# Cross-covariance attention on one core: one late store in column parts, three others head by head

## The chip, the core and the metric

The kernel runs on one core of a Trainium2 chip. The metric is device time in microseconds of one execution; the number given is the median of three runs. A run that is profiled besides leaves a trace: instructions of all engines, and the packets and landings of the transfers.

## The reference

For 8 batches of 12 heads, with 512 tokens and 64 features in float32, each head's features are normalised over the tokens, correlated with each other, passed through a softmax, and applied to V:

```
Q_norm = Q / (norm(Q, axis=-2) + 1e-10)          # over the 512 tokens
K_norm = K / (norm(K, axis=-2) + 1e-10)
attn = einsum('bhnd,bhne->bhde', Q_norm, K_norm) # 64 x 64 a head
attn = softmax(attn, axis=-1)
out  = einsum('bhnd,bhde->bhne', V, attn)
```

Q, K and V are 12.6 MB each, the output as much: 37.75 MB are read and 12.58 MB written.

## The kernel before

The 96 heads are worked in 12 steps (s = 0 to 11) of 8 heads, two steps to a pair w. A tile has 128 partitions: four heads with 32 partitions each, and a partition holds 16 tokens of each of two such groups of heads; the index r (0 or 1) tells the groups apart, and the kernel's text calls them heads. For each step the kernel loads 1 MB of Q and of K (`load_qk`, lines 219 and 221) and 1 MB of V (`load_v`, line 225), casts them to bf16, squares and sums for the norms, forms the Gram matrices on TensorE, scales them, takes the softmax, transposes V, multiplies, and copies the product from PSUM to an output tile `so[s]` (`ocopy`, line 205 on ScalarE). `so[s]` has the shape 128 x 2 x 16 x 64 (partition, r, token j, feature) in float32: 1 MB. In DRAM the 16 tokens of one partition and one r are 4096 bytes in a row, so a whole store is 256 rows of 4 KB.

The order of all pieces of work is planned ahead by the class `Order`, which lists them by costs, due times and ranks and emits them one by one; each engine then runs its own list in that order. All stores and nearly all loads are issued by SP (SyncE), one after the other. A transfer takes one of eight semaphores in turn, and its issue waits until the transfer that had this semaphore eight places before has landed. There are six output tiles, so that `so[s]` is used again by step s+6.

`store(s, i)` issues the store of step s, in one of three ways. For s = S - SPLIT = 9 it is split: PAR["CUTS"] has for each r the ranges of partitions that leave as transfers of their own, which are 0 to 68 and 68 to 128 for r=0, and all 128 for r=1 (line 232). All other steps leave as one transfer of 128 x 2 x 1024 (line 234), since the planner gives i = None for them. A store waits for the four copies into the part of `so[s]` that it reads. The last four stores, s = 8 to 11, are issued at 106.22, 109.13 (three parts), 111.42 and 114.83 us of the span, and their data wait in the queues of the 16 DMA engines behind what was issued earlier.

Of the kernel before, what the change touches and what calls it, by code (L numbers as in the profile page):

```python
# [13 lines left out]
PAR = {'NB': {'qk': 7, 'v': 3, 'vb': 2, 'qm': 2, 'sq': 2, 'vt': 2, 'so': 6, 'sm': 2, 'ab': 4},  # L14
 'TAIL': 3,
 'FINE': (0,),
 'ACTQ': True,
 'X': 1.27,
 'R': {'ck': 14.3601,
       'q': -46.9145,  # L20
       'sq': -4.5261,
       'sk': 21.309,
# [34 lines left out]
 'V_PACE': 0.7666,  # L57
 'ST_LAG': 6.0835,
 'SPLIT': 3,
 'CUTS': (((0, 68), (68, 128)), ((0, 128),))}  # L60

D = 64
T = 32
# [86 lines left out]
def kernel(  # L150
# [7 lines left out]
    nc = tc.nc  # L158
# [10 lines left out]
    Of = out.rearrange("b h (p j) d -> (b h p) (j d)", j=TT).rearrange("(w r e p) x -> w e p r x", r=2, e=2, p=128)  # L169
# [28 lines left out]
    qk32, qkb, sq, v32, vb, gram, st, s2, nn, r12, kqs, lg, ls, ex, ab, vps, vt, po, so = ({} for _ in range(19))  # L198
# [27 lines left out]

    def store(s, i):
        if s == S - PAR["SPLIT"]:
            for r in range(2):
                o, y = Of[s // 2, s % 2, :, r], so[s][:, r].rearrange("p j d -> p (j d)")  # L230
                for a, b in PAR["CUTS"][r]:
                    nc.sync.dma_start(out=o[a:b], in_=y[a:b])
        elif i is None:
            nc.sync.dma_start(out=Of[s // 2, s % 2], in_=so[s].rearrange("p r j d -> p r (j d)"))
        else:
            nc.sync.dma_start(out=Of[s // 2, s % 2, :, i], in_=so[s][:, i].rearrange("p j d -> p (j d)"))
# [232 lines left out]
    for s in range(S):  # L469
        for x in range(4):  # L470
            n = 4 * s + x - 2
            wait = [("oc", n // 4, n % 4)] if n >= 0 else []
            order = [("ou", s, x - 1) if x else back("ou", s, 1, 3)]
            piece(("ou", s, x), {"PE": 0.56}, [("vc", s // 2, *t) for t in turns(s // 2) if t[0] == x] + [("nm", s)] + wait, order, R["ou"] + 0.01 * s, outs, s, x)
            free = ([("st", s - NB["so"], i) for i in halves(s - NB["so"])] if x == 0 and s >= NB["so"] else [])
            order = [("oc", s, x - 1) if x else back("oc", s, 1, 3)]
            piece(("oc", s, x), {"ACT": 0.6, "DVE": 0.69}, [("ou", s, x)] + free, order, R["oc"] + 0.01 * s, ocopy, s, x)
        last = None
        for i in halves(s):
            order = [("st", s, 0) if i else ("st", s - 1, halves(s - 1)[-1]) if s else None]  # L480
            piece(("st", s, i), {"DMA": 2 * X if i is None else X}, [("oc", s, x) for x in range(4)], order, v_at(0.5 * s) + PAR["ST_LAG"], store, s, i)
# [35 lines left out]
```

## Time and profile before

| | |
|---|---|
| median of three runs | 128.31 us (128.14 to 128.37) |
| the profiled execution | 128.12 us |
| its span, first to last instruction | 126.0 us |
| busy: PE, DVE, ACT, POOL | 65%, 63%, 67%, 37% of the span |
| moved by DMA | 50.59 MB, mean 402 GB/s |
| transfers of SP and ACT (q1 and q10) | 95.3% and 2.0% of 16 engines' span |
| issued stores | 11 of 1024 KB, one of 512, 272 and 240 KB |
| time to landing of a 1024 KB store | 17.4 us median |

The span is the time from the first to the last instruction of the profiled execution; its own time has a start and an end around that. Shares of DMA are shares of 16 DMA engines; a fully loaded window reads slightly above 1, since the records of consecutive packets overlap a little. Engine names are PE (TensorE), DVE (VectorE), ACT (ScalarE), POOL (GpSimd) and SP (SyncE), with a q behind the name for an engine's queue of instructions. L232 is line 232 of the kernel. A landing is the time at which a transfer's semaphore was raised; it is raised once by each DMA engine that took part.

### The profile page before, as it was taken

The page shows a single profiled execution, that of the slowest core. Times are in us where ns is not written, and L with a number is a line of the kernel's source. Part 1 is how long each engine was busy: PE and PEld are TensorE (multiplying, and loading weights), DVE is VectorE, ACT ScalarE, POOL GpSimd, SP SyncE. Part 2 cuts the span into 40 slices and gives each one's busy share as a digit, 9 for nine tenths or more (in the row PEclk, how much of TensorE's full clock was granted, in tenths as well). Part 3 has the DMA queues.
Part 4 walks back from the last instruction along what each step waited for, and adds up shares of the span by engine and source line. Part 5 has one row for each costly group of instructions (what it writes and reads, how often), then busy time and mean ns, then how long its engine had stood idle before and what let it go on. Part 6 is the DMA issues. An engine that isn't in the chain of part 4 may idle for free.

```text
span 126.0 us, 4061 instructions
## 1 busy us (share of the span) xinstructions
PE 81.7 (65%) x1800; PEld 54.2 (43%) x1800; DVE 79.4 (63%) x140; ACT 85.0 (67%) x116; POOL 46.5 (37%) x40
## 2 busy tenths in 40 slices
PE   0009459894598787869578898864799878951000
PEld 0006145571474465557335556451387446630000
DVE  2223343899853989988987599993789998700000
ACT  4086668595697854998799987929839885864000
POOL 3250665470637098062707916144324700000000
PEclk9999999999657999995959999998559999996555
DMA  3999999999999999999999999999999999999982
GB/s 107 416 420 428 432 411 423 421 419 414 430 415 428 416 427 412 419 414 427 414 436 415 416 419 412 442 399 421 433 416 416 411 420 411 419 412 423 406 359 85
DMA packets 11588, 50.59 MB, mean 402 GB/s; under 512 B 819, under 2 KB 819, under 8 KB 10035
## 3 DMA queue, kind: packets, MB, share of 16 engines
q1 hardware_dynamic: 11283, 49.29, 95.3%
q10 hardware_dynamic: 288, 1.05, 2.0%
q8 instruction: 14, 0.23, 0.6%
q14 instruction: 3, 0.02, 0.0%
HBM read 37.75 MB, written 12.58 MB: 399 GB/s over the span
## 4 chain that ended last, share of the span: by engine, by line
DMA 54%; PE 15%; DVE 11%; ACT 6%; SPq 3%; issue 2%; ACTq 0%
DMA qk<-in_Q_dram 31%; DMA v<-in_V_dram 17%; DMA qk<-in_K_dram 6%; PE po L338 4%; ACT so L205 3%; PE l L266 3%; PE gram L260 3%; SPq L225 3%; DVE ab L310 2%; PE vps L323 2%; PE gram L289 2%; DVE s L271 1%; ACT sq L251 1%; DVE vt L207 1%; ACT vb L205 1%
## 5 line engine op out<-in xcount | busy, mean ns | idle before, releaser
L209 POOL TENSOR_SCALAR kb<-qk 128x2048 bf16<-128x2048 f32 (+1 forms) x13 | 23.4, 1802 | 38.1 <-DMA qk<-in_K_dram 35.0
L205 ACT COPY so<-po 128x512 f32<-128x512 f32 x47 | 25.6, 583 | 4.0 <-PE po L338 2.9
L251 ACT ACTIVATE sq<-qb 128x2048 bf16<-128x2048 bf16 (+1 forms) x13 | 23.1, 1778 | 7.7 <-DVE qb L207 7.6
L209 POOL TENSOR_SCALAR vb<-v 128x1024 bf16<-128x1024 f32 x15 | 20.1, 1355 | 13.7 <-DMA v<-in_V_dram 13.7
L338 PE MATMUL po<-ab,vt 128*32 128x128 bf16 x768 | 21.0, 237 | 6.0 <-ACT ex L299 1.6
L260 PE MATMUL gram<-qb,kb 32*128 32x128 bf16 x768 | 15.6, 240 | 12.2 <-POOL kb L209 9.6
L266 PE MATMUL l<-sq,hm 128*32 128x512 bf16 x96 | 19.5, 470 | 1.7 <-ACT sq L251 1.1
L323 PE MATMUL vps<-ident,vb 128*128 128x128 f32 x96 | 17.2, 305 | 4.4 <-POOL vb L209 2.3
L207 DVE CAST qb<-qk 128x2048 bf16<-128x2048 f32 (+1 forms) x12 | 13.6, 1135 | 10.0 <-DMA qk<-in_Q_dram 9.9
L260 PEld LDWEIGHTS <-kb 32*128 32x128 bf16 x768 | 13.4, 106 | 14.3 <-POOL kb L209 10.9
L338 PEld LDWEIGHTS <-vt 128*32 128x32 bf16 x768 | 14.3, 103 | 12.0 <-issue 7.7
L207 DVE COPY vt<-vps 128x1024 bf16<-128x1024 bf16 (+1 forms) x25 | 16.5, 664 | 3.0 <-PE vps L323 2.8
L251 ACT ACTIVATE sq<-kb 128x2048 bf16<-128x2048 bf16 (+1 forms) x10 | 17.3, 1734 | 0.7 <-POOL kb L209 0.7
L205 ACT CAST vb<-v 128x1024 bf16<-128x1024 f32 x9 | 12.1, 1344 | 6.8 <-DMA v<-in_V_dram 6.6
L323 PEld LDWEIGHTS vps<-ident,vb 128*128 128x128 f32 x96 | 11.3, 152 | 8.2 <-POOL vb L209 3.1
L271 DVE TENSOR_REDUCE s<-l 64x128 f32<-64x512 f32 x12 | 8.1, 678 | 8.5 <-PE l L266 8.5
L289 PE MATMUL gram<-ident,kqs 128*128 128x128 f32 x48 | 9.7, 336 | 3.5 <-DVE kqs L285 3.1
L295 DVE TENSOR_TENSOR ls<-gram,r 64x256 f32<-64x256 f32 x24 | 10.1, 420 | 2.7 <-PE gram L289 2.5
L285 DVE TENSOR_TENSOR kqs<-gram,r 128x512 f32<-128x512 f32 x12 | 8.2, 687 | 3.2 <-ACT r L281 2.6
L266 PEld LDWEIGHTS <-hm 128*32 128x32 bf16 x96 | 5.7, 108 | 9.7 <-issue 7.8
L310 DVE TENSOR_TENSOR ab<-ex,rb 128x512 bf16<-128x512 f32 x12 | 9.4, 781 | 0.4
L289 PEld LDWEIGHTS gram<-ident,kqs 128*128 128x128 f32 x48 | 6.2, 166 | 7.5 <-DVE kqs L285 6.6
(25 smaller groups left out, 41.3 us busy)
## 6 DMA issues: line engine op xcount, KB each, us to landing
v<-in_V_dram SPq DMA_DIRECT2D x12, 1024.0 KB, 19.5
qk<-in_Q_dram SPq DMA_DIRECT2D x11, 1024.0 KB, 19.6
qk<-in_K_dram SPq DMA_DIRECT2D x11, 1024.0 KB, 19.7
out_dram<-so SPq DMA_DIRECT2D x11, 1024.0 KB, 17.4
qk<-in_K_dram ACTq DMA_DIRECT2D x2, 512.0 KB, 6.0
qk<-in_Q_dram SPq DMA_DIRECT2D x2, 512.0 KB, 5.7
out_dram<-so SPq DMA_DIRECT2D x1, 512.0 KB, 10.0
out_dram<-so SPq DMA_DIRECT2D x1, 272.0 KB
```

The lines of the kernel that those rows point to most:

```text
L205: nc.scalar.copy(o, i)
L207: nc.vector.tensor_copy(o, i)
L209: nc.gpsimd.tensor_scalar(out=o, in0=i, scalar1=1.0, scalar2=0.0, op0=ALU.mult, op1=ALU.add)
L251: nc.scalar.activation(o, i, AF.Square)
L260: nc.tensor.matmul(gram[s][:, h, 0], k, q, start=(t == 0), stop=(t == TT - 1))
L266: nc.tensor.matmul(st[s][32 * x:32 * (x + 1)].rearrange("p t d -> p (t d)"), hm, sq[s][:, x, t:t + 4].rearrange("p t r d -> p (t r d)"), s ...
L271: nc.vector.tensor_reduce(out=s2[s], in_=st[s].rearrange("p t d -> p d t"), axis=mybir.AxisListType.X, op=ALU.add)
L289: nc.tensor.transpose(gram[s][:, h, 1], kqs[s][:, h], ident)
L295: nc.vector.tensor_tensor(out=ls[s][half], in0=gram[s][half, :, 1, half], in1=r12[s][half, :HU, None].to_broadcast([D, HU, D]), op=ALU.mult)
L310: nc.vector.tensor_tensor(out=ab[s], in0=ex[s][:, :, None, :].to_broadcast([128, HU, 2, D]), in1=rb[:, :, :, None].to_broadcast([128, HU, ...
L323: nc.tensor.transpose(ps[:, n], vb[w][:, j].rearrange("p r d c -> p (r d c)").bitcast(F32), ident)
L338: nc.tensor.matmul(po[s, x][32 * h:32 * (h + 1), j].rearrange("p r d -> p (r d)"), v, ab[s][:, h].rearrange("p r d -> p (r d)"), start=Tru ...
```

## The change

The split store of s=9 is cut anew, by tokens as well as partitions. A cut is now (r, first token, end token, first partition, end partition): tokens 0 to 6 of r=0 leave for the partitions 0 to 124 and 124 to 128 apart, then tokens 6 to 16 of r=0 for all 128 partitions, and then r=1 whole. The stores of the steps 8, 10 and 11 leave in two transfers each, first r=0 and then r=1. The planner doesn't know of this, and its order is unchanged. SP issues four transfers more; the lists of the other engines stay as they are.

```diff
  'SPLIT': 3,
- 'CUTS': (((0, 68), (68, 128)), ((0, 128),))}
+ 'HALF': (8, 10, 11),
+ 'CUTS': ((0, 0, 6, 0, 124), (0, 0, 6, 124, 128), (0, 6, 16, 0, 128), (1, 0, 16, 0, 128))}
...
     def store(s, i):
         if s == S - PAR["SPLIT"]:
+            for r, j0, j1, a, b in PAR["CUTS"]:
+                nc.sync.dma_start(out=Of[s // 2, s % 2, a:b, r, j0 * D:j1 * D], in_=so[s][a:b, r, j0:j1].rearrange("p j d -> p (j d)"))
+        elif s in PAR["HALF"]:
             for r in range(2):
-                o, y = Of[s // 2, s % 2, :, r], so[s][:, r].rearrange("p j d -> p (j d)")
-                for a, b in PAR["CUTS"][r]:
-                    nc.sync.dma_start(out=o[a:b], in_=y[a:b])
+                nc.sync.dma_start(out=Of[s // 2, s % 2, :, r], in_=so[s][:, r].rearrange("p j d -> p (j d)"))
         elif i is None:
             nc.sync.dma_start(out=Of[s // 2, s % 2], in_=so[s].rearrange("p r j d -> p r (j d)"))
```

The new rows of s=9 are 1536 bytes long for the tokens 0 to 6, and 2560 bytes for the tokens 6 to 16; together they are the 4096 bytes of before.

## The prediction

> **What bounds the kernel now.** I read the page first (engines, slices), then the chain of waits, then the waits of SP's queue, then single transfers and narrow time windows at the end. No engine is busy for more than 67% of the span, while the DMA line stands at 9 from the second slice on:
>
> ```profile
> PE 81.7 (65%) x1800; PEld 54.2 (43%) x1800; DVE 79.4 (63%) x140; ACT 85.0 (67%) x116; POOL 46.5 (37%) x40
> ...
> DMA  3999999999999999999999999999999999999982
> ```
>
> The chain's last piece of computing is the copy of the last output tile, and what SP waits for after that is only the landing of stores:
>
> ```profile
> 114.22 0.58 ACT so L205
> ```
>
> ```profile
> SPq L512 <- DMA out_dram<-so: 9.7, 1, 9.7
> ```
>
> So computing ends at 114.80 us and the last 11 us are the DMA engines emptying what is queued. The span ends 1.1 us after the last landing (below). What can shorten this kernel here is only how evenly the last megabytes lie over the 16 DMA engines. Time windows of that stretch (columns: window, its length, busy PE, PEld, DVE, ACT, POOL, granted clock, share of the 16 DMA engines, GB/s):
>
> ```profile
> 119.00:120.00 1.00, 0.00 (x0) 0.00 (x0) 0.00 (x0) 0.00 (x0) 0.00 (x0) 0.50 1.02 418
> ...
> 121.00:121.50 0.50, 0.00 (x0) 0.00 (x0) 0.00 (x0) 0.00 (x0) 0.00 (x0) 0.50 0.86 352
> ...
> 122.50:123.00 0.50, 0.00 (x0) 0.00 (x0) 0.00 (x0) 0.00 (x0) 0.00 (x0) 0.50 0.72 295
> ...
> 123.50:124.00 0.50, 0.00 (x0) 0.00 (x0) 0.00 (x0) 0.00 (x0) 0.00 (x0) 0.50 0.29 115
> 124.00:124.50 0.50, 0.00 (x0) 0.00 (x0) 0.00 (x0) 0.00 (x0) 0.00 (x0) 0.50 0.08 33
> ```
>
> A full load reads 1.02. So three engines run dry before 121 us, two more before 122.5, most of the rest between 123.5 and 124, and one or two are left in the last half microsecond. The trace's landing records, one time for each DMA engine of a transfer, say it exactly. The last store (s=11) lands on three engines at 121.04 to 121.19, on two at 122.71 and 122.80, on nine at 123.90 to 124.25, and on two alone at 124.64 and 124.89. The two late ones are what the change can reach.
>
> **Whose engines they are.** Store s=9, the one that is cut, was issued in three parts; SP's timeline gives their start, the DMA issues their size and time to landing:
>
> ```profile
> 109.13 1.18 SPq L232 DMA_DIRECT2D out_dram<-so  x3
> 111.42 3.79 SPq L234 DMA_DIRECT2D out_dram<-so  x2
> ```
>
> ```profile
> out_dram<-so SPq DMA_DIRECT2D x1, 512.0 KB, 10.0
> out_dram<-so SPq DMA_DIRECT2D x1, 272.0 KB
> out_dram<-so SPq DMA_DIRECT2D x1, 240.0 KB, 9.1
> ```
>
> In the landing records the 68-row part has 4 engines' landings (117.08, 117.21, 117.73, 117.80; the other 12 counts come with the issue at 109.58, hence no time in the list), the 60-row part 15, a 128-row part 16. That is the greatest divisor of the rows that is not above 16. So in s=9 four engines ("the four") carry 17+4+8 = 29 rows of 4 KB, eleven carry 4+8 = 12, and one carries 8. Store s=8 before it had landed on seven engines at 114.32 to 115.14, three at 115.84 to 115.94 and six at 117.06 to 117.45. The four start from the early seven (117.08 less 17 rows is 114.4, 117.80 less 17 rows is 115.2), and followed through 60-row part, second head, s=10 and s=11, two of them are the stragglers: 117.80, 118.66, 119.92, 122.40, 124.89, and 117.73, 118.41, 119.66, 122.16, 124.64. The six late engines of s=8 are in the nine and end at up to 124.25. Today the four have been given about half a microsecond too much.
>
> **Price of a row.** The packet records give 159 ns for 4096 bytes, 309 ns for 8192 and 9 ns for a completion: 9 ns a packet and 150 ns per 4 KB. Consecutive packets overlap a little: 16 rows with their completion take 2.49 us (118.92 to 121.41 to 123.90), 155.4 ns a row. So I take 5.4 + 150 x bytes/4096 ns: 61.7 ns for 1536 bytes, 99.2 for 2560, 155.4 for 4096. No row of 1536 or 2560 bytes is in this trace. The lower bound is bytes alone (58.3 and 97.1), the upper within this line the whole packet time (65.3 and 102.8); a rival below goes beyond it.
>
> **The change, part by part.**
>
> *Cut of s=9.* 124 and 4 rows go to 4 engines each by the same count: 31+1 rows of 1536 bytes, then 8 rows of 2560 and 8 of 4096 on all 16. The four: 32 x 61.7 + 8 x 99.2 + 8 x 155.4 = 1.97 + 0.79 + 1.24 = 4.01 us, against 29 x 155.4 = 4.51: 0.50 less (bounds 0.43 to 0.62). The eleven: 0.79 + 1.24 = 2.04 against 12 x 155.4 = 1.86: 0.17 more (0.16 to 0.19). The one: 2.04 against 1.24, 0.79 more, hidden: it belongs to the three that end at 121.
>
> The Trainium skill, "DMA: Bandwidth & Descriptors", section "Why a DMA increments its semaphore by 16 and not by 1", has the same count of engines for 68, 60 and 128 rows as the landing records, and adds what no record here names, that SP's transfers take the lowest-numbered engines, so that both pieces would fall on the four that the 68-row part used; by that the sum stays at 127.87.
>
> *Stores 8, 10 and 11 by heads, and one part more in s=9.* The bytes per engine are the same, and rows stay 4 KB. Added are three completions on most engines, four on the four, 9 ns each: 0.03 and 0.04 us. A gap between two transfers is not seen: 8 rows of the second head of s=9 took 1.24 us from landing to landing, half of the 2.49 of a whole store. SP issues four more transfers (0.33 to 0.40 us each), while it would wait anyway. The semaphore of each transfer is reused eight transfers later, so now the last ones wait for nearer landings: s=10's heads for s=6 and s=7 (112.40 and 114.91, where s=10 left at 111.42), s=11's heads for the two heads of s=8 (about 116.2 and 117.45, where s=11 left at 114.83). Nothing stands behind them on SP but the end. What hides this is the queue: from the first issue to its first packet it takes 1.0 us (0.74 to 1.75), so the last head is ready by about 118.9 with its issue, and the emptiest engine needs it at 114.32 + 2.04 + 2.49 + 1.24 = 120.1, the late ones at 123.2. If that cover were gone, each microsecond of late issue past it would count in full. Cost taken: nothing. The instructions of PE, DVE, ACT and POOL are the same in the same order; the output tiles of these stores are not reused.
>
> *Sum.* Stragglers: 124.89 - 0.50 + 0.04 = 124.43. The late engines: 124.25 + 0.17 + 0.03 = 124.45, now the last. The end moves from 124.89 to 124.45: 0.44 us (0.39 to 0.49 by the bounds; what a cheaper row would give beyond this, the late engines keep). The profiled execution took 128.12 us (126.0 span, 2.1 around it), so 127.68; the median of the runs lies 0.19 above that execution: **127.87**.
>
> The Trainium skill speaks against the change, in "DMA: Bandwidth & Descriptors", section "Rules for kernel authors": small transfers should be joined, and below 64 KB one pays mostly overhead; the first head's 4-row piece is 6 KB. The 60-row part of 240 KB shows none of it here (landings 0.62 us after s=8's on the late engines, four rows' time), but no run here shows a 6 KB one.
>
> **The rivals.**
>
> *Late engines alone set the end.* One straggler lost 0.25 us at 115.76, where a foreign packet of 8 KB (314 ns, the instruction queue q14) fell on it. If that falls elsewhere in ordinary runs, before ends at 124.64 there, after still at 124.45: a gain of 0.2, 128.1. For it: the runs spread by 0.23 us. Against: the profiled execution has the packet and is no slower than they are.
>
> *Short rows cost more than their bytes (slower).* Place: the 32 rows of 1536 bytes on the four. From 76 ns a row on the stragglers end after 124.89. At 100 ns they take 3.20 instead of 1.97 us: 129.1; if every packet cost as much as one of 4 KB, 48 x 155.4 = 7.46 against 4.51: 131.3. For it: no such row is measured. Against: the 4096, 8192 and 4-byte packets lie on one line.
>
> *The pieces land on other engines (slower).* If they fell on four of the late ones, those would carry 4.05 instead of 1.86 us and end at 126.4: 129.9. Nothing in the trace hints at a rotation, but it has one such transfer only.
>
> *The added transfers leave gaps (slower).* Where a transfer began only as after an idle queue, 1.0 us each, three more on the late engines would give 131.3; from 0.15 us each on it is slower. Against: a share of 1.02 across all the boundaries from 114 to 120 us. This is what the rule on small transfers of the Trainium skill ("DMA: Bandwidth & Descriptors", "Rules for kernel authors") would amount to.
>
> *The 124 rows are spread over 16 engines after all,* so the change does not shift load as said: the late ones get 8 x 61.7 ns more and end near 124.95: 128.4, no change.
>
> **How the numbers follow.** Less than 0.2% (0.26 us) can't be told from no change. Forecast 0.64; late engines alone 0.14; short rows 0.08; other engines 0.05; gaps 0.05; spread 0.04. Faster: the forecast and a part of the second, 0.67; same: 0.14; slower: 0.19. The range: the forecast's own is 127.7 to 128.0 with the runs' spread; up to 128.5 it takes in the second and the last rival and mildly dear rows, down to 127.6 a foreign packet that falls well.
>
> **What would show it.** Right: the last landing at about 124.45, all four parts of s=9 with landings on 4, 4, 16 and 16 engines, packets of 1536 bytes at about 65 ns, eleven or more engines ending within half a microsecond, and a steeper fall of the DMA share after 123.5. Wrong: packets of 1536 bytes above 85 ns; a share below 1 between 114 and 120 us; stragglers among the engines that were late in s=8 by more than 0.2 us; s=11's second head issued later than 119.

## The result, and the profile after

The changed kernel takes 127.55 us (median of six runs, 127.52 to 127.77), the kernel before 128.16 us beside it (six runs, 128.02 to 128.37): the ratio is 0.9953, with a 95% interval from 0.9940 to 0.9966. That is faster by 0.61 us, where 0.44 was forecast, and 0.05 us below the lower end of the range. The profiled execution took 127.52 us with a span of 125.4, against 128.12 and 126.0. Ratios and their intervals, here and below, are worked out from the single runs and not from the two medians, so they can differ from the quotient of the medians. Two slow runs, one of e1_cut_only (130.20 us) and one of the kernel before (130.32 us, beside e5 to e7), are left out of them.

The page after shows the same picture: no engine busy for more than 68%, and the DMA line full but for its ends.

```profile
PE 77.8 (62%) x1800; PEld 52.3 (42%) x1800; DVE 81.1 (65%) x140; ACT 84.8 (68%) x116; POOL 47.0 (37%) x40
...
DMA  2999999999999999999999999999999999999993
```

The chain of waits ends with the same copy, at 114.82 us (114.80 before), so nothing was gained ahead of the last stores:

```profile
114.23 0.59 ACT so L206
```

The time windows of the end (window, length, busy engines, granted clock, share of 16 DMA engines, GB/s):

```profile
119.00:120.00 1.00, 0.00 (x0) 0.00 (x0) 0.00 (x0) 0.00 (x0) 0.00 (x0) 0.50 1.03 422
...
121.00:121.50 0.50, 0.00 (x0) 0.00 (x0) 0.00 (x0) 0.00 (x0) 0.00 (x0) 0.50 0.94 385
...
122.50:123.00 0.50, 0.00 (x0) 0.00 (x0) 0.00 (x0) 0.00 (x0) 0.00 (x0) 0.50 0.71 287
...
123.50:124.00 0.50, 0.00 (x0) 0.00 (x0) 0.00 (x0) 0.00 (x0) 0.00 (x0) 0.50 0.50 205
124.00:124.50 0.50, 0.00 (x0) 0.00 (x0) 0.00 (x0) 0.00 (x0) 0.00 (x0) 0.50 0.03 8
```

Before, the share was 0.29 from 123.5 to 124 and 0.08 after that: by the landing records, two engines were left over. Now it is 0.50 and then 0.03: more engines work to the end, and they stop nearly together. By the landing records the last head of s=11 lands on three engines at 121.56 to 121.99, two at 122.96 and 123.11, the four at 123.55, 123.61, 124.13 and 124.35, and seven at 124.40 to 124.55. The last landing came 0.34 us earlier (124.89 to 124.55).

The span, however, became 0.60 us shorter, so another 0.26 us lies behind the last landing. SP's own waits show where (waiting line, releaser, us in total, times, longest):

```profile
SPq L514 <- DMA out_dram<-so: 6.5, 5, 1.8
```

Before it was one wait of 9.7 us. At its end SP checks the eight transfer semaphores with five waiting instructions, always in the same order. Before, the last store's semaphore was in the first of them: SP waited there until 124.91, and then the other four, all long satisfied, ran at 124.98, 125.05, 125.11 and 125.17. The four transfers that were added move the last store on to the semaphore in the fifth: the first four waits are done at 119.66, 120.88, 122.09 and 123.32, while the queue is still emptying, and only one is left at 124.56. The span ends 0.84 us behind the last landing instead of 1.10.

SP's timeline of the end and its DMA issues, to be held against those that the prediction shows of the kernel before:

```profile
106.93 0.85 SPq L234 DMA_DIRECT2D out_dram<-so  x2
108.28 2.58 SPq L231 DMA_DIRECT2D out_dram<-so  x4
112.63 5.25 SPq L234 DMA_DIRECT2D out_dram<-so  x4
```

```profile
out_dram<-so SPq DMA_DIRECT2D x7, 512.0 KB, 8.2
out_dram<-so SPq DMA_DIRECT2D x1, 320.0 KB, 8.7
out_dram<-so SPq DMA_DIRECT2D x1, 186.0 KB
out_dram<-so SPq DMA_DIRECT2D x1, 6.0 KB
```

The pieces of 186 and 6 KB have no landing time in the list, like the 272 KB piece of before: in the landing records each of the three has landings of 4 engines only.

### The profile page after: what moved, and what is told of

Same layout as the page of the kernel before. It is cut to its first block, busy times and chain, and to the rows that moved or that the text cites. A ratio compares the mean times of both kernels' runs of the same rounds, so it can differ in the third digit from the quotient of the medians.

```text
span 125.4 us, 4066 instructions
## 1 busy us (share of the span) xinstructions
PE 77.8 (62%) x1800; PEld 52.3 (42%) x1800; DVE 81.1 (65%) x140; ACT 84.8 (68%) x116; POOL 47.0 (37%) x40
## 4 chain that ended last, share of the span: by engine, by line
DMA 54%; PE 15%; DVE 9%; ACT 7%; SPq 3%; issue 2%; POOL 1%; ACTq 0%
DMA qk<-in_Q_dram 31%; DMA v<-in_V_dram 17%; DMA qk<-in_K_dram 6%; PE l L268 4%; ACT so L206 4%; PE po L340 3%; PE gram L262 3%; PE vps L325 3%; SPq L226 3%; PE gram L291 2%; ACT sq L253 1%; DVE ab L312 1%; DVE sq L255 1%; DVE ls L297 1%; DVE vt L208 1%
## 5 line engine op out<-in xcount | busy, mean ns | idle before, releaser
L340 PE MATMUL po<-ab,vt 128*32 128x128 bf16 x768 | 20.2, 232 | 6.3 <-DVE ab L312 2.6
L268 PE MATMUL l<-sq,hm 128*32 128x512 bf16 x96 | 17.8, 450 | 2.7 <-ACT sq L253 2.6
L325 PE MATMUL vps<-ident,vb 128*128 128x128 f32 x96 | 16.7, 297 | 4.3 <-DVE vt L208 2.1
L325 PEld LDWEIGHTS vps<-ident,vb 128*128 128x128 f32 x96 | 10.8, 147 | 8.2 <-DVE vt L208 2.9
L291 PE MATMUL gram<-ident,kqs 128*128 128x128 f32 x48 | 9.1, 319 | 4.5 <-DVE kqs L287 4.3
L312 DVE TENSOR_TENSOR ab<-ex,rb 128x512 bf16<-128x512 f32 x12 | 11.4, 950 | 0.4
L291 PEld LDWEIGHTS gram<-ident,kqs 128*128 128x128 f32 x48 | 5.7, 155 | 8.5 <-DVE kqs L287 7.7
```

Source lines behind the costliest of these rows:

```text
L268: nc.tensor.matmul(st[s][32 * x:32 * (x + 1)].rearrange("p t d -> p (t d)"), hm, sq[s][:, x, t:t + 4].rearrange("p t r d -> p (t r d)"), s ...
L291: nc.tensor.transpose(gram[s][:, h, 1], kqs[s][:, h], ident)
L312: nc.vector.tensor_tensor(out=ab[s], in0=ex[s][:, :, None, :].to_broadcast([128, HU, 2, D]), in1=rb[:, :, :, None].to_broadcast([128, HU, ...
L325: nc.tensor.transpose(ps[:, n], vb[w][:, j].rearrange("p r d c -> p (r d c)").bitcast(F32), ident)
L340: nc.tensor.matmul(po[s, x][32 * h:32 * (h + 1), j].rearrange("p r d -> p (r d)"), v, ab[s][:, h].rearrange("p r d -> p (r d)"), start=Tru ...
```

## The experiments

The theory after the result ("two-term theory"): the cut brings the last landing forward by balance, and the number of transfers brings the end of the span nearer to the last landing by the order of SP's final waits. Its rivals: all of it comes from the cut ("queue theory"), or from the stores by heads ("heads theory"). Each kernel is compared with the kernel before on the same chip. The diffs are against the changed kernel and show the entries of PAR that differ.

### Only the cut (e1_cut_only)

```diff
- 'HALF': (8, 10, 11),
+ 'HALF': (),
```

> Only the new cut of s=9; the stores 8, 10 and 11 leave whole. Two-term theory (the last landing comes 0.34 us earlier by the cut, and the end of the span comes nearer to the last landing where the last store's semaphore is among the last that SP checks at the end): the last store's semaphore is here in the second of the five final waits, three more follow at 0.065 us each, so the last landing is at 124.4 to 124.55 us and the span ends 1.04 us behind it (before 1.10, after 0.85); the time is 0.40 us below the kernel before (0.35 to 0.50), ratio 0.997. Queue theory (all 0.6 us come from the cut's balance, and the end is as it falls): ratio 0.9953 as with the whole change. Heads theory (the stores by heads bring the gain): ratio 1.000.

Measured: 127.68 us against 128.13, ratio 0.9956 (0.9940 to 0.9971). The last landing is at 124.59, and the span ends 1.03 us behind it. SP's waits:

```profile
SPq L514 <- DMA out_dram<-so: 9.0, 2, 6.6
```

Two waits that blocked, then three that ran through. The end behind the last landing is that of the two-term theory (expected 1.04); the last landing is 0.04 later than the expected 124.4 to 124.55. The heads theory falls: its 1.000 is outside the interval. By time alone, 0.45 us lies between the 0.40 of the two terms and the 0.6 of the queue theory, and the interval holds both. The last landing without the stores by heads is nearly as early as with them (124.59, against 124.55).

### Only the stores by heads (e2_heads_only)

```diff
- 'CUTS': ((0, 0, 6, 0, 124), (0, 0, 6, 124, 128), (0, 6, 16, 0, 128), (1, 0, 16, 0, 128))}
+ 'CUTS': ((0, 0, 16, 0, 68), (0, 0, 16, 68, 128), (1, 0, 16, 0, 128))}
```

> The stores 8, 10 and 11 by heads, but s=9 cut as before (68 and 60 rows, then 128). Two-term theory: last landing at 124.9 us as before (plus 0.03 for three completions), and the last store's semaphore is in the fourth of the five final waits, so the span ends 0.92 us behind the last landing: 0.15 us below the kernel before (0.1 to 0.2), ratio 0.9988. Queue theory: ratio 1.000. Heads theory: 0.9953.

Measured: 128.05 us against 128.13, ratio 0.9986 (0.9965 to 1.0006), with single runs from 127.66 to 128.88. The span ends 0.90 us behind the last landing, as expected:

```profile
SPq L514 <- DMA out_dram<-so: 8.2, 4, 4.6
```

The last landing was at 125.37 in its profiled execution, 0.45 later than expected, and that execution (128.38 us) was the second longest of the twelve: fifteen engines were done by 124.35, and one of the four came a microsecond later. It had left s=8 late (115.30) and then had two packets of 474 and 352 ns instead of 159 in the 60-row part. The time can't tell 0 from 0.15 us; the heads theory's 0.9953 is outside the interval.

### The cut with the last store back in the first wait (e3_cut_first_wait)

```diff
- 'HALF': (8, 10, 11),
+ 'HALF': (4, 5, 6, 7, 8, 10, 11),
```

> The whole change, and the stores 4 to 7 by heads as well. That puts the last store's semaphore back into the first of the five final waits, as in the kernel before, and leaves the load of every DMA engine as in the changed kernel. Two-term theory: last landing at 124.45 to 124.6, the span ends 1.10 us behind it, the time is 0.26 us above the changed kernel: 0.35 us below the kernel before, ratio 0.9973. Queue theory: ratio 0.9953 as with the whole change, the end behind the last landing 0.85.

Measured: 127.86 us against 128.13, ratio 0.9971 (0.9960 to 0.9983). Last landing 124.69, the span's end 1.10 us behind it, and again one wait only:

```profile
SPq L514 <- DMA out_dram<-so: 6.7, 1, 6.7
```

This is the cleanest test of the second term: the load that s=9 puts on each engine is that of the changed kernel, the end behind the last landing is that of the kernel before to the hundredth, and the queue theory's 0.9953 is outside the interval. The time alone would not show it: of the 0.40 us by which this span is longer than the changed kernel's, 0.26 lie behind the last landing and 0.14 before it, since the last landing came 0.09 later than the expected 124.45 to 124.6.

### The old cut with the last store in the last wait (e4_old_cut_last_wait)

```diff
- 'HALF': (8, 10, 11),
- 'CUTS': ((0, 0, 6, 0, 124), (0, 0, 6, 124, 128), (0, 6, 16, 0, 128), (1, 0, 16, 0, 128))}
+ 'HALF': (6, 7, 8, 10),
+ 'CUTS': ((0, 0, 16, 0, 68), (0, 0, 16, 68, 128), (1, 0, 16, 0, 128))}
```

> The kernel before, with the stores 6, 7, 8 and 10 by heads and nothing else changed: the cut of s=9 is the old one and s=11 leaves whole. The last store's semaphore is then in the last of the five final waits. Two-term theory: last landing at 124.9 us as before, the span ends 0.85 us behind it, 0.22 us below the kernel before (0.15 to 0.3), ratio 0.9983. Queue theory: ratio 1.000, the end 1.10 us behind the last landing.

Measured: 127.82 us against 128.13, ratio 0.9972 (0.9961 to 0.9983), from runs of 127.77 to 127.89. Last landing 124.86 (124.89 before), with two stragglers as before (124.84 and 124.86); the end 0.83 us behind it:

```profile
SPq L514 <- DMA out_dram<-so: 9.2, 5, 3.1
```

The second term alone, with the old balance, is worth 0.27 us at the end of the span. The medians differ by 0.31.

### The balance in its size: even, and too much (e5_even, e6_more_on_four)

```diff
- 'CUTS': ((0, 0, 6, 0, 124), (0, 0, 6, 124, 128), (0, 6, 16, 0, 128), (1, 0, 16, 0, 128))}
+ 'CUTS': ((0, 0, 16, 0, 128), (1, 0, 16, 0, 128))}
```

> The changed kernel without the shift of load: s=9 leaves in two whole heads, 8 rows of 4096 bytes on every engine each. By the prices of the prediction the four engines carry 16 x 155.4 = 2.49 us instead of 4.01, the late ones 2.49 instead of 2.04. Two-term theory: the late engines land last, 0.45 us later than in the changed kernel, at 125.0, the four at 122.0 to 122.9; the last store's semaphore is in the third of the five final waits, the end 0.97 us behind the last landing: 0.57 us above the changed kernel, about level with the kernel before, ratio 1.000. A theory in which the cut only adds transfers and the balance is worth nothing: as the changed kernel plus the 0.13 us of the final waits, ratio 0.9965.

Measured: 128.06 us against 128.24, ratio 0.9981 (0.9958 to 1.0003). Last landing 124.94, expected at 125.0 by the late engines; seven engines end at 121.77 to 122.75, where the four were expected at 122.0 to 122.9 (no record of this run tells the four apart); the end is 0.96 us behind, with three waits:

```profile
SPq L514 <- DMA out_dram<-so: 9.0, 3, 6.6
```

The landing is close to where the row prices put it, 0.39 us behind the changed kernel's (0.45 expected), so the balance is worth that much against even stores. The ratio's interval holds both theories; it is the landings that decide.

```diff
- 'CUTS': ((0, 0, 6, 0, 124), (0, 0, 6, 124, 128), (0, 6, 16, 0, 128), (1, 0, 16, 0, 128))}
+ 'CUTS': ((0, 0, 12, 0, 124), (0, 0, 12, 124, 128), (0, 12, 16, 0, 128), (1, 0, 16, 0, 128))}
```

> The changed kernel with 12 tokens instead of 6 in the pieces of 124 and 4 rows, so rows of 3072 and 1024 bytes. By the price line of the prediction (5.4 ns + 150 ns per 4 KB) the four engines carry 32 x 117.9 + 8 x 42.9 + 8 x 155.4 = 5.36 us instead of 4.01, the late ones 0.34 + 1.24 = 1.58 instead of 2.04. Two-term theory: the four land last, at 125.7 (124.35 + 1.35), the late ones at 124.1, the end 0.84 us behind: 1.15 us above the changed kernel, ratio 1.0043. If the pieces went to other engines than the early four, or rotated between them, the last landing would be elsewhere: above 127.5.

Measured: 128.55 us against 128.24, ratio 1.0004 (0.9977 to 1.0030), which is 1.0 us above the changed kernel's 127.55, where 1.15 was expected. The expected 1.0043 is outside the interval: beside the 0.15, the kernel before had a median 0.08 higher here, and single runs of up to 129.47 us lower the ratio further (the two medians alone give 1.0024). In the trace the four land last at 124.83, 125.00, 125.47 and 125.59 (expected 125.7), the late engines at 123.95 to 124.07 (expected 124.1), the end 0.83 us behind. The windows show the four alone at the end, at 0.26 of 16 engines:

```profile
124.00:124.50 0.50, 0.00 (x0) 0.00 (x0) 0.00 (x0) 0.00 (x0) 0.00 (x0) 0.50 0.26 107
```

So the four late landings are where load on the early four puts them, and not where other engines or a rotation would. Packets of 3072 and 1024 bytes took 121 and 46 ns; 9 ns and 150 ns per 4 KB give 121.5 and 46.5.

### Which engines come next (e7_seven), and a try at a better version (e8_four_and_six)

```diff
- 'CUTS': ((0, 0, 6, 0, 124), (0, 0, 6, 124, 128), (0, 6, 16, 0, 128), (1, 0, 16, 0, 128))}
+ 'CUTS': ((0, 0, 6, 0, 119), (0, 0, 6, 119, 128), (0, 6, 16, 0, 128), (1, 0, 16, 0, 128))}
```

> The changed kernel with 119 and 9 rows instead of 124 and 4: by the count seen so far the 119 rows go to 7 engines with 17 rows each, the 9 rows to 9 engines with one each. It tells which engines come behind the four in order. Four landings of the 119 rows at 115.7 to 116.4 (the early four, 17 x 61.7 = 1.05 us behind s=8). The other three show their class: early (115.7), middle (117.0) or late (118.4). If one of the three is late, the last landing is 1.05 us later than the late engines' in the changed kernel, at 125.6, ratio 1.003 (I take this for likelier); if none is, the last landing stays at 124.5 and the time at that of the changed kernel, and a version with five or more engines may beat it.

Measured: 128.36 us against 128.24, ratio 0.9994 (0.9968 to 1.0019). The 119 rows have seven landings: 115.50, 115.66, 116.14 and 116.38 (the four), 116.83 and 116.86 (two middle ones), 118.53 (a late one). The late one ends at 125.57 (expected 125.6), all others by 124.50. The landings came nearly as expected (the first 0.2 earlier than 115.7), the ratio did not: 1.003 is outside the interval. The median is 0.81 above the changed kernel's, and the profiled execution, 128.54, was the longest of ten.

```diff
- 'HALF': (8, 10, 11),
- 'CUTS': ((0, 0, 6, 0, 124), (0, 0, 6, 124, 128), (0, 6, 16, 0, 128), (1, 0, 16, 0, 128))}
+ 'HALF': (8,),
+ 'CUTS': ((0, 0, 2, 0, 124), (0, 0, 2, 124, 128), (0, 2, 9, 0, 114), (0, 2, 9, 114, 128), (0, 9, 16, 0, 128), (1, 0, 16, 0, 128))}
```

> A version meant to beat the changed kernel. The seven engines of the run with 119 rows fell into the early four, two middle ones and one late one. Here the first head of s=9 leaves as 2 tokens by 124 and 4 rows (4 engines), 7 tokens by 114 and 14 rows (6 and 14 engines), 7 tokens by 128; only s=8 goes by heads, so that the last store stays in the last of the five final waits. By the price line the four carry 4.00 us in s=9 (4.01 in the changed kernel), engines five and six 3.23 instead of 2.04, the rest 1.88 instead of 2.04. If engines five and six are the two middle ones: last landing 124.4, 0.15 us before the changed kernel's 124.55, the end 0.84 us behind, ratio to the kernel before 0.994. If one of them is the late one: last landing 125.7, ratio 1.004. Queue theory without the order of the final waits: the same landings, but no statement on the end.

Measured: 128.36 us against 128.26, ratio 0.9998 (0.9980 to 1.0017). The 114 rows have six landings, the last at 118.55: the late engine is one of these six. It ends alone at 125.35, while the other fifteen are done by 124.19. For this case 125.7 and a ratio of 1.004 were expected, and 1.004 is outside the interval; the late engines had left s=8 at up to 117.26 here, 0.26 earlier than in the changed kernel. So the version does not beat the changed kernel. The landings of 4, 6 and 7 engines fit one growing set, in which the late one stands before the second of the two middle ones; a set of five was not tried.

### The changed kernel again (e9_changed_again)

The kernel is unchanged, beside the last one on the same chip.

> The changed kernel as it is, beside the run above on the same chip. Two-term theory: last landing at 124.45 to 124.6, the end 0.84 us behind it, ratio 0.9953 as in the first comparison. If its first gain was a chance of the seat of foreign packets, 0.998 or above.

Measured: 127.40 us against 128.26, ratio 0.9921 (0.9895 to 0.9947). Last landing 124.63 (0.03 later than expected), the end 0.83 us behind it. The gain is there again, larger than expected: 0.9953 is outside the interval. That comes in part from the runs of the kernel before, which here spread from 127.93 to 128.99; the rest, a median 0.15 below the first one, is open.

## Why the prediction was right and where it was wrong

**Right: what bounds the end, and who carries what.** The 124 and 4 rows landed on 4 engines each, the other two parts of s=9 on 16. The Trainium skill ("DMA: Bandwidth & Descriptors", section "Why a DMA increments its semaphore by 16 and not by 1") counts engines by the greatest divisor up to 16; 119, 114 and 14 rows give 7, 6 and 14 by it. The trace agrees: 7, 6 and 14 landings for these rows.

**Right: the price of short rows.** Packets of 1536 and 2560 bytes took 65 and 102 ns, where 65.3 and 102.8 were the whole packet times. The four needed 3.95 to 4.05 us for s=9 (114.62 to 118.58, 115.35 to 119.40), forecast 4.01; the last of the late engines 2.12 (117.52 to 119.64), forecast 2.04. The short-rows rival is out. The sum came out better than its terms: on the first of the four the 32 short rows took 2.02 us to their landing (1.97 forecast) and the 8 rows of 2560 bytes 0.69 (0.79).

**Right: nothing of the added transfers and waits is late.** SP issued the last heads at 112.63, 115.16, 116.35 and 117.54, against a forecast of 112.40, 114.91, 116.2 and 117.45, and the DMA share stays at 1.02 or above until 121 us. The 6 KB piece landed 0.18 us behind the 124 rows (116.46 to 116.64), where its one row and completion were priced at 0.07; by the next landing, 0.69 us later, this was made up. The Trainium skill's rule against transfers under 64 KB ("DMA: Bandwidth & Descriptors", "Rules for kernel authors") names a cost that a full queue did not pass on here.

**Mis-sized: the last landing.** It came at 124.55 instead of 124.45, by the late engines as forecast. They came out of s=8 at up to 117.52 instead of 117.45, and needed 0.08 more for s=9 and 0.07 less for the four heads behind it (4.91 instead of 4.98). So the gain by balance was 0.34 us, not 0.44, and lies below the 0.39 to 0.49 that the prediction gave as bounds. The other executions with the new cut landed at 124.59, 124.63 and 124.69: 0.34 is the most of four. The stragglers met their forecast by luck (124.35, against 124.43): the last of them left s=8 0.21 us later than before, and the old cut had cost it 4.78 us (115.14 to 119.92) and not 4.51, for a reason given below.

**Wrong: the end behind the last landing.** The step that failed is the one sentence "The span ends 1.1 us after the last landing (below)", and the sum that took this as fixed: it put the change of this term at nothing, without a reason. It went from 1.10 to 0.84 us. Over all kernels it is 0.83 to 1.10 us, by the place of the last store's semaphore among the five final waits. The prediction had seen that the semaphores go round by eight and used it for the issues of s=10 and s=11, but not for the end; and the row it showed, one wait of 9.7 us, fits a block on the first of several. The profiles, each of one execution:

| blocking final waits | kernel | last landing | end behind it |
|---|---|---|---|
| 1 | before | 124.89 | 1.10 |
| 1 | e3_cut_first_wait | 124.69 | 1.10 |
| 2 | e1_cut_only | 124.59 | 1.03 |
| 3 | e5_even | 124.94 | 0.96 |
| 4 | e2_heads_only | 125.37 | 0.90 |
| 5 | after | 124.55 | 0.84 |
| 5 | e4_old_cut_last_wait | 124.86 | 0.83 |

The kernels e6 to e9 also have five such waits, and their ends are at 0.83 to 0.84. Each place is worth 0.065 us ((1.10 - 0.84) / 4), whatever the cut.

**Wrong: the step from the profiled execution to the median.** It was taken as 0.19 us, from three runs. The changed kernel's median is 0.03 above its profiled execution, the kernel before's 0.04 once six runs are taken (128.16, against 128.12), and in the later comparisons it had medians from 128.13 to 128.26. The account from 127.87 to 127.55: final waits -0.26, last landing +0.10, this step -0.16. Neither the final waits nor this step would have led out of the range alone (127.61 and 127.71 without the other terms); together they did. That 0.61 lies near 0.44 is in part luck: the balance gave less than forecast, by 0.10, and the final waits, which were not forecast, gave 0.26.

**Wrong: what delayed one straggler.** The second rival put its 0.25 us down to a foreign packet at 115.76. The straggler's 68-row part was not delayed then; its own packet at 117.95, in the 60-row part, took 380 instead of 159 ns. The other profiles with the old cut have such a packet in the same place (332 ns at 117.97 in e4_old_cut_last_wait, 474 in e2_heads_only). Whether the 60-row part on 15 engines causes it was not tried.

**Slips that moved nothing.** In the rival of gaps, three gaps of 1.0 us on the late engines end at 127.45 and so at 130.9, not 131.3. The upper bound 0.49 of the gain doesn't come out of the prediction's prices: with bytes alone the late engines end at 124.44, a gain of 0.45. And the share of 1.02 "across all the boundaries from 114 to 120 us" was 1.00 from 117 to 118.

## What to carry to other kernels

When a kernel ends in a full queue, follow each DMA engine's landings, not the transfers': in these runs the row count of a store decided how many engines shared it (4 for 68 and 124 rows, 7 for 119, 16 for 128), and so let one shift load between them. Read the time behind the last landing as a term of its own: a single long wait at the end, where several are checked in order, can mean that the rest still has to run, and here each transfer more or less moved the last one's place, by 0.065 us. Splitting a transfer can thus gain or lose time at a spot that has nothing to do with its bytes.

## What the runs showed of the hardware

The DMA engines of one core drift apart. In the kernel before, 16 landings of one transfer lie within 0.5 us at 22.5 us of the span but for one straggler at 24.27, and within 3.1 us at 114.3 to 117.5. Of the 14 packets of 16 KB on the instruction queue (q8, 879 to 967 ns), the first eight are each followed by one more engine 1.4 to 1.9 us behind the earliest: one after the packet at 21.7, two after that at 29.9, eight by 81 us. After the next packet, at 81.8, one engine is 3.2 us behind. The four that the small row counts reach left s=8 among the early engines in every trace that has their landings. That the packets cause the lag is read from the order of times; no run took them away.
